# An attention block in split float32: who makes the lo parts of the weights, the squares of the outputs, and the product with the gate

## The chip, the cores and the metric

The kernel runs on one core of one Trainium2 chip. The metric is the device time of the whole program in microseconds, the median of several executions. A profiled execution also leaves a trace with every instruction of the five engines: TensorE (PE, with its weight loads as PEld), VectorE (DVE), ScalarE (ACT), GpSimd (POOL) and SyncE (SP, which only issues transfers here).

## What is computed

One transformer block over 512 tokens of width 2048, in float32. A projection of the normed input gives the inputs of four groups of 8 heads each: a latent attention (MLA), a causal attention with forget gates (FoX), a sparse attention with three branches (NSA) and a sliding window with sinks (SWA). Their outputs are normed by group, projected by `w_out` and added to the input; an MLP with a squared ReLU and a last norm follow. Cut to what matters here:

```python
def nsa_mixer(...):
    o_cmp, o_sel = nsa_cmp_sel(qg, k_cmp, v_cmp, ksl, vsl, tbl)
    o_win = banded_attention(qg, kwn, vwn, NSA_WINDOW, tbl)
    gts = jax.nn.sigmoid(gate).reshape(b, t, g, r, 3).transpose(0, 2, 3, 1, 4)
    o = gts[..., 0:1] * o_cmp + gts[..., 1:2] * o_sel + gts[..., 2:3] * o_win

def reference(...):
    u = rmsnorm(h, norm_attn[l])
    p = jnp.split(u @ w_in[l], offsets, axis=-1)
    ...
    o = jnp.concatenate([o_mla, o_fox, o_nsa, o_swa], axis=-1).reshape(b, t, N_GROUPS, GROUP_WIDTH)
    o = rmsnorm(o, group_norm[l].reshape(N_GROUPS, GROUP_WIDTH)).reshape(b, t, MIX_WIDTH)
    h = h + o @ w_out[l]
    m = rmsnorm(h, norm_mlp[l]) @ w_up[l]
    h = h + jnp.square(jax.nn.relu(m)) @ w_down[l]
    return rmsnorm(h, final_norm)
```

## The kernel before

A float32 product is made of three products in a shorter float format: each factor x is split into hi (x rounded to that format) and lo (x - hi, rounded again), and TensorE adds hi·hi, hi·lo and lo·hi in PSUM.

Weights come in pieces. `piece` (line 204) takes a raw tile of 128 x 1024 from a transfer on SyncE's queue (three raw buffers), lets ScalarE cast it to `hi` (line 210), and lets the engine in `lo_engine` subtract to get `lo` (line 211). `hi` and `lo` have two buffers each, in the arena `hl`. `lo_engine` is VectorE for the first projections (until about 115 us) and GpSimd from line 604 on. That holds 82 pieces: the projections to queries, keys and values that run inside the attention, and the output projection.

The attention runs as a list of steps, one for each block of 128 queries of a head, in the order MLA, NSA, FoX, SWA. TensorE's order is written out by hand: scores of step i, some products of a projection that has been cut in small portions (`pull`), transposes of the probabilities of step i-1 (line 565), more portions, and the values of step i-2 (line 571). The order of the other engines is left to a planner that follows the dependencies with a cost model; `nc.any` copies (line 518) go to VectorE or ScalarE as the planner sees fit. Every engine works through its queue in order.

`soft` (line 497) makes the probabilities: VectorE adds the bias to the scores in PSUM and finds the negated maximum `nm` (line 503), ScalarE takes the exponential with its sum `l` (line 506), VectorE takes the reciprocal `r` (line 511), multiplies it by the gate (through the helper `tt`, line 136) where the branch has one, and scales the row by it (line 514). Two branches of the NSA pass a gate, 64 blocks in all. The compressed branch has code of its own.

`finish_head` copies a head's output to `oT`; after the second head of a pair `add_squares` (line 529) squares the pair's tile of 128 x 512 and adds it to its group's sum `sqs`, on GpSimd. `group_rstd` reads the sum some steps into a later phase. There are 16 such tiles in four groups, so 16 squares and 12 additions.

GpSimd's queue holds besides these a few masks and the transfers that carry the residual to and from DRAM (lines 1249 and 1345).

Of the kernel before, what the change touches and what calls it, by code (L numbers as in the profile page):

```python
# [10 lines left out]
F32 = mybir.dt.float32  # L11
F32R = mybir.dt.float32r
BF16 = mybir.dt.bfloat16
AF = mybir.ActivationFunctionType
ALU = mybir.AluOpType
# [60 lines left out]
def block(tc, a, out):  # L76
    nc = tc.nc
    pool = tc.tile_pool
    with (
# [29 lines left out]
        def tl(shape, dt, tag, bufs=1):  # L109
            if tag not in plan:  # L110
                return sb.tile(shape, dt, tag=tag, name=tag, bufs=bufs)
            slots, size, used = plan[tag]
            arena, off = slots[used[0] % len(slots)]
            off //= 4
            used[0] += 1
            free = list(shape[1:])
            m = math.prod(free)
            assert (2 if dt == BF16 else 4) * m <= size, tag
            if dt == BF16:
                t = arena[0:shape[0], off:off + m // 2].bitcast(BF16)  # L120
            else:
                assert dt == arena.dtype, tag
                t = arena[0:shape[0], off:off + m]
            if len(free) == 2:
                t = t.rearrange("p (a b) -> p a b", b=free[1])
            elif len(free) == 3:
                t = t.rearrange("p (a b c) -> p a b c", b=free[1], c=free[2])
            elif len(free) == 4:
                t = t.rearrange("p (a b c d) -> p a b c d", b=free[1], c=free[2], d=free[3])
            return t  # L130
# [4 lines left out]
        def tt(o, x, y, op):  # L135
            nc.vector.tensor_tensor(o, x, y, op=op)  # L136
# [48 lines left out]
        def small(shape, tag, bufs=4):  # L185
            return tl(shape, F32, tag, bufs)
# [12 lines left out]
            return y  # L199


        lo_engine = [nc.vector]

        def piece(fills, used=1024):
            raw = tl([P, 1024], F32, "raw")
            for f in fills:
                f(raw)
            hi = tl([P, 1024], F32R, "hi")
            lo = tl([P, 1024], F32R, "lo")
            nc.scalar.copy(hi[:, 0:used], raw[:, 0:used])  # L210
            lo_engine[0].tensor_tensor(lo[:, 0:used], raw[:, 0:used], hi[:, 0:used].bitcast(F32), op=ALU.subtract)  # L211
            return hi, lo

        def w_piece(w, r0, kt, c0, n):

            def fill(raw):
                nc.sync.dma_start(raw[:, 0:kt * n].rearrange("p (k c) -> p k c", c=n),
                                  w[r0:r0 + kt * P, c0:c0 + n].rearrange("(k p) c -> p k c", p=P))
            return piece([fill], kt * n)
# [43 lines left out]
        def proj_tok(segs, n, before=lambda pc: None):  # L263

            accs = [ps("acc") for _ in range(TB)]
            for pc in range(8):
                before(pc)
                def fill(raw, pc=pc):
                    off = 0
                    r = raw[:, 0:2 * n].rearrange("p (k c) -> p k c", c=n)  # L270
                    for c0, w in segs:
                        nc.sync.dma_start(r[:, :, off:off + w],
                                          w_in[pc * 256:(pc + 1) * 256, c0:c0 + w].rearrange("(k p) c -> p k c", p=P))
                        off += w
                wh, wl = piece([fill], 2 * n)
                for b in range(TB):
                    for k in range(2):
                        kt = pc * 2 + k
                        for j, (w, u) in enumerate(three(wh, wl, uh[kt], ul[kt])):
                            mm(accs[b][:, 0:n], lhsT=u[:, b * P:(b + 1) * P], rhs=w[:, k * n:(k + 1) * n],  # L280
                               start=(kt == 0 and j == 0), stop=(kt == KT - 1 and j == 2))
            return accs
# [40 lines left out]
        for k in range(4):  # L323
            t = ps("s")
            for b in range(TB):
# [4 lines left out]
                                           op1=ALU.subtract)  # L330
# [166 lines left out]
        def soft(S, W, bias, sink=None, mul=None):  # L497

            p = tl([P, 512], F32, "tp")
            nm = small([P, 1], "nm")  # L500
            l = small([P, 1], "l")
            r = small([P, 1], "r")
            nc.vector.tensor_tensor_reduce(p[:, 0:W], S[:, 0:W], bias, scale=-1.0,  # L503
                                           scalar=big if sink is None else sink[1], op0=ALU.add, op1=ALU.min,
                                           accum_out=nm)
            nc.scalar.activation(p[:, 0:W], p[:, 0:W], AF.Exp, bias=nm, scale=-1.0, accum_out=l)  # L506
            if sink is not None:
                e = small([P, 1], "es")
                nc.scalar.activation(e, sink[0], AF.Exp, bias=nm)
                tt(l, l, e, ALU.add)  # L510
            nc.vector.reciprocal(r, l)
            if mul is not None:
                tt(r, r, mul, ALU.mult)
            nc.vector.tensor_scalar_mul(p[:, 0:W], p[:, 0:W], r)  # L514
            return p

        def evac(o, i):
# [2 lines left out]
        oT = [None] * 16  # L520
        sqs = {}
# [7 lines left out]
        def add_squares(n):  # L529

            if n % 4 == 0:
                sqs[n // 4] = tl([P, T], F32, "sqs")
                nc.gpsimd.tensor_tensor(sqs[n // 4], oT[n], oT[n], op=ALU.mult)
            else:
                sq = tl([P, T], F32, "tp")
                nc.gpsimd.tensor_tensor(sq, oT[n], oT[n], op=ALU.mult)
                nc.gpsimd.tensor_tensor(sqs[n // 4], sqs[n // 4], sq, op=ALU.add)

        def group_rstd(g):

# [60 lines left out]
        def fill_v(raw):  # L601
            nc.sync.dma_start(raw[:, 0:512].rearrange("p (h c) -> p h c", c=64), w_ukv_h[:, :, 64:128])
        wh, wl = piece([fill_v], 512)
        lo_engine[0] = nc.gpsimd
        vm = tl([P, TB, 512], F32, "acc2")
        for b in range(TB):
            acc = ps("acc")
# [61 lines left out]
        def mla_head(h):  # L669
            def score(i):  # L670
                W = (i + 1) * P

                def f(head):
                    Qh, Ql, Kh, Kl = kept[f"mla{h}"]
                    S = ps("s")
                    for j, (q, k) in enumerate(three(Qh, Ql, Kh, Kl)):
                        mm(S[:, 0:W], lhsT=q[:, i * P:W], rhs=k[:, 0:W], start=(j == 0), stop=(j == 2))
                    return soft(S, W, causal[:, 512 - W:512])
                return Block(f, W, lambda kb: vm[:, kb, h * 64:(h + 1) * 64], range(i + 1), i, 3 * W / 2.4)

            return Head(h // 2, h % 2, [score(i) for i in range(TB)], lambda: require(f"mla{h}"))
# [445 lines left out]
        with tc.manual_schedule(engines={mybir.EngineType.PE}):  # L1127
# [5 lines left out]
            for i in range(len(steps) + 2):  # L1133
# [15 lines left out]
                if i >= 2:  # L1149
                    head, _, j = steps[i - 2][:3]  # L1150
                    n = len(head.blocks)
# [289 lines left out]
        for j0, j1 in zip(GROUPS, GROUPS[1:]):  # L1441
            n, ms = j1 - j0, ready
# [115 lines left out]
```

## Time and profile before

| | |
|---|---|
| median of 3 executions | 2196.44 us (2195.49 to 2198.48) |
| profiled execution, its own time | 2199.35 us |
| span of the profile, first to last instruction | 2197.6 us |
| mean granted TensorE clock | 0.994 |
| PE busy | 2139.2 us, 97% |
| DVE busy | 1685.0 us, 77% |
| ACT busy | 1013.5 us, 46% |
| POOL busy | 247.8 us, 11% |

Busy times are of one profiled execution. An engine's instruction is busy from its start to its end, also while something outside it holds it up. TensorE's ends are modelled. A granted clock of 1.00 is 2.4 GHz, one of 0.50 is 1.2 GHz. Times in the rows count from the first instruction.

### The profile page before, as it was taken

The numbers are of one execution on the slowest core, as the hardware profiler recorded it, in microseconds if no ns is written. First come the engines' busy times: TensorE is split into PE (matmuls) and PEld (weight loads), VectorE is DVE, ScalarE is ACT, GpSimd is POOL, SyncE is SP. The second block draws the span as 40 slices with busy tenths as digits, with TensorE's granted clock in tenths as the row PEclk, the third lists the DMA queues.
The fourth block names the chain that finished last, engine by engine and source line by source line (L and its number), as shares of the span: only waits on it lengthen the run. The fifth ranks groups of instructions, "written<-read, shape, count | busy, mean of one in ns | idle before, by whom it ended". The sixth has DMA issues, their size and how long they took to land.

```text
span 2197.6 us, 37520 instructions
## 1 busy us (share of the span) xinstructions
PE 2139.2 (97%) x14441; PEld 1927.2 (88%) x14441; DVE 1685.0 (77%) x3118; ACT 1013.5 (46%) x1646; POOL 247.8 (11%) x152
## 2 busy tenths in 40 slices
PE   8999999999999998999999999999999999999998
PEld 6778777777778787999999999999999999999996
DVE  3466755665576657888888888888788888889997
ACT  4354433434455525654444444446544444444434
POOL 0011322323333343100000000000000000000000
PEclk9999999999999999999999999999999999999999
DMA  6452222222233233655544544456544544544553
GB/s 184 119 152 70 76 61 78 68 71 76 69 120 101 68 96 128 200 186 165 164 163 145 167 164 163 143 167 221 192 131 153 176 139 150 175 142 147 169 178 114
DMA packets 244815, 299.27 MB, mean 136 GB/s; under 512 B 28268, under 2 KB 199327, under 8 KB 239900
## 3 DMA queue, kind: packets, MB, share of 16 engines
q1 hardware_dynamic: 231424, 246.60, 37.4%
q10 hardware_dynamic: 11228, 41.87, 4.9%
q0 software_dynamic: 1984, 8.41, 1.1%
q8 instruction: 113, 1.85, 0.3%
q14 instruction: 66, 0.54, 0.1%
HBM read 254.70 MB, written 49.46 MB: 138 GB/s over the span
## 4 chain that ended last, share of the span: by engine, by line
PE 82%; DVE 9%; DMA 3%; issue 3%; ACT 2%; POOL 0%; ACTq 0%; SPq 0%; DVEq 0%; POOLq 0%
PE acc L1293 22%; PE s L1293 13%; PE acc L423 9%; PE t L1293 6%; PE acc L973 6%; PE acc L1397 4%; PE acc L280 4%; PE o L571 3%; PE o L1293 3%; PE s L1397 2%; PE acc L894 2%; PE t L565 2%; DVE tpp L514 1%; PE o L1397 1%; PE t L1397 1%
## 5 line engine op out<-in xcount | busy, mean ns | idle before, releaser
L423 PE MATMUL acc<-u,hl 128*128 128x512 f32 x1008 | 282.0, 411 | 0.0
L211 POOL TENSOR_TENSOR hl<-raw,hl 128x1024 fp32r<-128x1024 f32 x82 | 197.3, 2406 | 456.6 <-ACT hl L210 394.7
L1293 PE MATMUL acc<-u,acc 128*128 128x256 f32 x1162 | 233.2, 281 | 0.6 <-DVE ka L1400 0.6
L1287 ACT CAST acc<-raw 128x896 fp32r<-128x896 f32 x146 | 136.7, 941 | 178.5 <-PE t L1293 79.6
L1287 ACT CAST acc<-bx 128x896 fp32r<-128x896 f32 x146 | 136.8, 941 | 173.2 <-PE acc L1293 71.1
L1287 ACT CAST acc<-tpp 128x896 fp32r<-128x896 f32 x144 | 134.7, 941 | 175.9 <-PE acc L1293 70.5
L423 PEld LDWEIGHTS acc<-u,hl 128*128 128x128 f32 x1008 | 177.4, 191 | 34.5 <-issue 4.8
L973 PE MATMUL acc<-hl,u 128*128 128x512 f32 x768 | 195.0, 401 | 5.0 <-DVE acc L981 2.3
L1293 PEld LDWEIGHTS acc<-u,acc 128*128 128x128 f32 x1162 | 186.5, 188 | 1.0 <-DVE ka L1400 0.8
L506 ACT ACTIVATE tpp<-tpp,nm 128x256 f32<-128x256 f32 (+3 forms) x160 | 86.5, 541 | 184.9 <-DVE nm L503 176.1
L973 PEld LDWEIGHTS acc<-hl,u 128*128 128x128 f32 x768 | 139.2, 189 | 35.5 <-DVE acc L981 3.0
L210 ACT CAST hl<-raw 128x1024 fp32r<-128x1024 f32 (+2 forms) x99 | 102.3, 1033 | 136.7 <-PE acc L973 46.3
L1293 PE MATMUL acc<-ot,acc 128*128 128x256 f32 x714 | 152.1, 283 | 3.4 <-ACT acc L1287 3.4
L1293 PE MATMUL s<-u,acc 128*128 128x256 f32 x664 | 134.6, 281 | 0.0
L1293 PE MATMUL acc<-acc,acc 128*128 128x256 f32 x476 | 133.8, 281 | 0.0
L1293 PEld LDWEIGHTS acc<-ot,acc 128*128 128x128 f32 x714 | 118.3, 190 | 3.8 <-ACT acc L1287 3.6
L136 DVE TENSOR_TENSOR bx<-bx 128x256 f32<-128x256 f32 (+1 forms) x219 | 111.6, 510 | 11.6 <-DMA bx<-in_w_up_dram 4.3
L136 DVE TENSOR_TENSOR tpp<-tpp 128x256 f32<-128x256 f32 (+1 forms) x222 | 114.6, 517 | 6.5 <-DMA tpp<-in_w_up_dram 1.9
L136 DVE TENSOR_TENSOR raw<-raw 128x256 f32<-128x256 f32 (+1 forms) x219 | 111.6, 509 | 9.4 <-DMA raw<-in_w_down_dram 5.6
L1293 PEld LDWEIGHTS s<-u,acc 128*128 128x128 f32 x664 | 106.4, 188 | 0.0
L1293 PE MATMUL acc<-u,u 128*128 128x256 f32 x371 | 103.9, 280 | 0.0
L1288 DVE TENSOR_TENSOR ot<-raw,acc 128x896 fp32r<-128x896 f32 x72 | 78.1, 1088 | 20.2 <-ACT acc L1287 20.2
(683 smaller groups left out, 5946.3 us busy)
## 6 DMA issues: line engine op xcount, KB each, us to landing
m_dram<-ka ACTq DMA_DIRECT2D x32, 1024.0 KB, 5.2
raw<-in_w_in_dram SPq DMA_DIRECT2D x58, 512.0 KB, 3.9
bx<-in_w_up_dram SPq DMA_DIRECT2D x86, 256.0 KB, 2.8
raw<-in_w_up_dram SPq DMA_DIRECT2D x86, 256.0 KB, 2.8
tpp<-in_w_up_dram SPq DMA_DIRECT2D x84, 256.0 KB, 2.9
raw<-in_w_out_dram SPq DMA_DIRECT2D x32, 512.0 KB, 3.7
raw<-m_dram SPq DMA_DIRECT2D x30, 512.0 KB, 4.5
kb<-m_dram SPq DMA_DIRECT2D x30, 512.0 KB, 3.9
```

What stands on the lines that cost most here:

```text
L136: nc.vector.tensor_tensor(o, x, y, op=op)
L210: nc.scalar.copy(hi[:, 0:used], raw[:, 0:used])
L211: lo_engine[0].tensor_tensor(lo[:, 0:used], raw[:, 0:used], hi[:, 0:used].bitcast(F32), op=ALU.subtract)
L280: mm(accs[b][:, 0:n], lhsT=u[:, b * P:(b + 1) * P], rhs=w[:, k * n:(k + 1) * n], start=(kt == 0 and j == 0), stop=(kt == KT - 1 and j == 2))
L423: mm(acc[0], lhsT=x[:, k * P:(k + 1) * P], rhs=u, start=(kt == 0 and j == 0), stop=(kt == KT - 1 and j == 2))
L506: nc.scalar.activation(p[:, 0:W], p[:, 0:W], AF.Exp, bias=nm, scale=-1.0, accum_out=l)
L571: mm(o[r0:r0 + 64, self.i * P:(self.i + 1) * P], lhsT=self.V(kb), rhs=self.pt[:, j * P:(j + 1) * P], start=(first and j == 0), stop=(last ...
L973: mm(accs[b], lhsT=u[:, b * P:(b + 1) * P], rhs=x[:, k * 512:(k + 1) * 512], start=(hf == 0 and k == 0 and j == 0), stop=(hf == 1 and k == ...
L1287: nc.scalar.copy(wh, w[:, k, 0:7, :])
L1288: lo = nc.vector.tensor_tensor(wl, w[:, k, 0:7, :], wh.bitcast(F32), op=ALU.subtract)
L1293: mm(banks[bank][:, half * HT:(half + 1) * HT], lhsT=lhs, rhs=rhs, start=(start and k == 0 and i == 0 and half == 0), stop=(stop and k == ...
L1397: mm(acc, lhsT=y, rhs=x, start=(start and i == 0), stop=(stop and i == 2))
```

## The change

Three edits. The lo parts of all pieces are subtracted on VectorE, each in halves of up to 512 columns, and `lo_engine` goes. The squares of `add_squares` are taken by ScalarE and the additions by VectorE; GpSimd is left with masks, small copies and transfers. Where `soft` is given a gate, the reciprocal is no longer multiplied by it; the scaling takes both scalars, p · r · gate, in one instruction.

```diff
-        lo_engine = [nc.vector]
-
         def piece(fills, used=1024):
...
             nc.scalar.copy(hi[:, 0:used], raw[:, 0:used])
-            lo_engine[0].tensor_tensor(lo[:, 0:used], raw[:, 0:used], hi[:, 0:used].bitcast(F32), op=ALU.subtract)
+            for c in range(0, used, 512):
+                e = min(c + 512, used)
+                tt(lo[:, c:e], raw[:, c:e], hi[:, c:e].bitcast(F32), ALU.subtract)
             return hi, lo
...
             nc.vector.reciprocal(r, l)
-            if mul is not None:
-                tt(r, r, mul, ALU.mult)
-            nc.vector.tensor_scalar_mul(p[:, 0:W], p[:, 0:W], r)
+            if mul is None:
+                nc.vector.tensor_scalar_mul(p[:, 0:W], p[:, 0:W], r)
+            else:
+                nc.vector.tensor_scalar(p[:, 0:W], p[:, 0:W], r, mul, op0=ALU.mult, op1=ALU.mult)
             return p
...
             if n % 4 == 0:
                 sqs[n // 4] = tl([P, T], F32, "sqs")
-                nc.gpsimd.tensor_tensor(sqs[n // 4], oT[n], oT[n], op=ALU.mult)
+                nc.scalar.activation(sqs[n // 4], oT[n], AF.Square)
             else:
                 sq = tl([P, T], F32, "tp")
-                nc.gpsimd.tensor_tensor(sq, oT[n], oT[n], op=ALU.mult)
-                nc.gpsimd.tensor_tensor(sqs[n // 4], sqs[n // 4], sq, op=ALU.add)
+                nc.scalar.activation(sq, oT[n], AF.Square)
+                tt(sqs[n // 4], sqs[n // 4], sq, ALU.add)
...
         wh, wl = piece([fill_v], 512)
-        lo_engine[0] = nc.gpsimd
         vm = tl([P, TB, 512], F32, "acc2")
```

## Rows read from the trace of the kernel before

**Rows 1.** The page, parts 1 and 4: busy time of TensorE's matmuls (share of the span, instructions), and the shares of the engines in the chain of work that ended last.

```profile
PE 2139.2 (97%) x14441; PEld 1927.2 (88%) x14441; DVE 1685.0 (77%) x3118; ACT 1013.5 (46%) x1646; POOL 247.8 (11%) x152
...
PE 82%; DVE 9%; DMA 3%; issue 3%; ACT 2%; POOL 0%; ACTq 0%; SPq 0%; DVEq 0%; POOLq 0%
```

**Rows 2.** Busy time by stage. Columns: stretch, its length, then busy us and number of instructions for PE, PEld, DVE, ACT and POOL, then the granted TensorE clock as a share of full speed, the DMA engines' share, GB/s. The first four stretches are the attention by its phases, the fifth lies in the output projection, the last is the MLP.

```profile
124.00:260.00 136.00, 128.07 (x724) 105.49 (x723) 90.62 (x240) 61.14 (x153) 29.82 (x19) 0.97 0.35 93
260.00:440.00 180.00, 175.75 (x929) 138.71 (x928) 107.59 (x312) 73.17 (x163) 53.93 (x25) 0.99 0.26 70
440.00:645.00 205.00, 194.83 (x1066) 155.61 (x1067) 130.93 (x329) 92.50 (x202) 63.37 (x31) 1.00 0.29 82
645.00:770.00 125.00, 118.83 (x629) 97.17 (x628) 85.92 (x228) 65.96 (x180) 45.90 (x23) 1.00 0.29 88
...
840.00:860.00 20.00, 16.06 (x75) 12.29 (x74) 16.58 (x20) 9.44 (x14) 9.06 (x6) 0.98 0.21 74
...
905.00:2197.00 1292.00, 1280.41 (x9910) 1235.49 (x9908) 1128.10 (x1772) 606.46 (x741) 1.64 (x3) 1.00 0.50 162
```

**Rows 3.** TensorE's waits between 124 and 770 us: who waited for whom, us in total, times, the longest.

```profile
PE t L565 <- DVE tpp L514: 23.9, 18, 2.5
PE t L824 <- DVE r L136: 1.9, 2, 1.2
```

**Rows 4.** Groups of VectorE's and GpSimd's instructions by line and tile: count | busy us, mean ns | idle time of the engine before them. Line 136 is the helper `tt`, line 514 the scaling of probabilities.

```profile
L514 DVE TENSOR_SCALAR tpp<-tpp,r 128x256 f32<-128x256 f32 (+3 forms) x160 | 85.7, 536 | 4.0
...
L136 DVE TENSOR_TENSOR r<-r,gate 128x1 f32<-128x1 f32 x64 | 31.7, 496 | 1.8
...
L136 DVE TENSOR_TENSOR q<-ot,q 64x512 fp32r<-64x512 f32 x16 | 21.1, 1320 | 1.2 <-ACT q L459 0.7
...
L211 POOL TENSOR_TENSOR hl<-raw,hl 128x1024 fp32r<-128x1024 f32 x82 | 197.3, 2406 | 456.6 <-ACT hl L210 394.7 <-PE s L790 22.1 <-PE acc L423 20.8
```

**Rows 5.** Extremes of some of these instructions: count, least / median / greatest ns, first and last start in us, forms. The row of line 211 on VectorE holds the pieces of the first 124 us.

```profile
L136 DVE TENSOR_TENSOR r<-r,gate x64: 147/160/1876, 260.4 to 516.2; 128x1 f32<-128x1 f32 x64
...
L136 DVE TENSOR_TENSOR q<-ot,q x16: 677/687/2560, 246.5 to 703.9; 64x512 fp32r<-64x512 f32 x16
...
L514 DVE TENSOR_SCALAR tpp<-tpp,r x160: 270/382/2592, 128.5 to 768.8; 128x256 f32<-128x256 f32 x56, 128x128 f32<-128x128 f32 x40, 128x384 f32<-128x384 f32 x40, 128x512 f32<-128x512 f32 x24
...
L503 DVE CUSTOM_DVE_ANT_0 tpp<-s,bx,big x80: 333/541/751, 126.8 to 641.9; 128x384 f32<-128x384 f32 x24, 128x128 f32<-128x128 f32 x20, 128x256 f32<-128x256 f32 x20, 128x512 f32<-128x512 f32 x16
...
L211 DVE TENSOR_TENSOR hl<-raw,hl x17: 691/1093/1226, 11.6 to 113.4; 128x1024 fp32r<-128x1024 f32 x8, 128x896 fp32r<-128x896 f32 x8, 128x512 fp32r<-128x512 f32 x1
```

**Rows 6.** Instructions in order of time around 657 us, in the phase of the sliding windows: start us, us, engine, line, operation, tile; in brackets the idle time of the engine before it and what ended it.

```profile
653.35 0.34 DVE L514 TENSOR_SCALAR tpp<-tpp,r 128x256 f32<-128x256 f32 x1
...
655.48 1.03 ACT L210 CAST hl<-raw 128x1024 fp32r<-128x1024 f32 x1
...
656.58 2.52 DVE L514 TENSOR_SCALAR tpp<-tpp,r 128x256 f32<-128x256 f32 x1
656.59 2.36 POOL L211 TENSOR_TENSOR hl<-raw,hl 128x1024 fp32r<-128x1024 f32 x1 [3.71 <-ACT hl L210]
...
659.24 0.41 PE L565 MATMUL t<-ident,tpp 128*128 128x128 f32 x2 [1.75 <-DVE tpp L514]
```

**Rows 7.** The same view around 317 us, in the phase with the gate.

```profile
314.38 1.05 ACT L210 CAST hl<-raw 128x1024 fp32r<-128x1024 f32 x1 [2.50 <-issue]
...
316.07 0.16 DVE L511 RECIPROCAL r<-l 128x1 f32<-128x1 f32 x1 [0.63 <-ACT tpp L506]
...
316.26 1.64 DVE L136 TENSOR_TENSOR r<-r,gate 128x1 f32<-128x1 f32 x1
...
318.36 0.41 DVE L514 TENSOR_SCALAR tpp<-tpp,r 128x384 f32<-128x384 f32 x1
...
318.92 0.52 PE L565 MATMUL t<-ident,tpp 128*128 128x128 f32 x3 [1.74 <-DVE tpp L514]
```

**Rows 8.** Busy time as in rows 2, in short stretches; the granted clock is the third value from the end.

```profile
156.00:159.00 3.00, 3.00 (x14) 2.57 (x13) 2.74 (x7) 1.96 (x6) 0.14 (x1) 0.50 0.09 22
...
252.00:254.00 2.00, 2.00 (x8) 1.71 (x8) 0.76 (x4) 0.00 (x0) 0.00 (x0) 0.50 0.33 116
...
385.00:388.00 3.00, 3.00 (x10) 2.32 (x9) 0.91 (x4) 0.69 (x2) 0.00 (x0) 0.50 0.18 59
...
659.00:663.00 4.00, 3.76 (x23) 3.35 (x24) 3.22 (x15) 1.77 (x8) 0.00 (x0) 1.00 0.53 168
```

**Rows 9.** TensorE's own instructions in order of time, ahead of the first two of these stretches.

```profile
154.80 0.63 PE L565 MATMUL t<-ident,tpp 128*128 128x128 f32 x4 [2.23 <-DVE tpp L514]
...
251.03 0.52 PE L565 MATMUL t<-ident,tpp 128*128 128x128 f32 x3 [2.46 <-DVE tpp L514]
```

**Rows 10.** TensorE's instructions in the output projection.

```profile
857.15 0.49 PE L973 MATMUL acc<-hl,u 128*128 128x512 f32 x1 [1.73 <-POOL hl L211]
858.96 1.60 PE L973 MATMUL acc<-hl,u 128*128 128x512 f32 x3 [1.32 <-DVE acc L981]
```

**Rows 11.** ScalarE: the squares of the residual (line 983) as a group, and the waits of the cast that makes the hi parts (line 210) between 124 and 770 us.

```profile
L983 ACT ACTIVATE acc<-acc 128x512 f32<-128x512 f32 x12 | 7.2, 597 | 2.6 <-DVE acc L981 2.2 <-DVE l L136 0.2
...
ACT hl L210 <- issue: 24.4, 17, 3.6
...
ACT hl L210 <- PE acc L423: 8.9, 10, 2.0
```

## The prediction

> **What bounds the kernel now.** I read the page's busy shares and chain first, then a table by stage, then TensorE's waits, and then the neighbourhood of single waits. The page [rows 1] shows a kernel that is already TensorE's: it is busy for 97% of the span, and 82% of the chain that ended last lies on it. A change to VectorE, ScalarE and GpSimd can win only what TensorE stands idle for or does at a lower clock. The table by stage [rows 2] says where that is. From 905 us to the end (the MLP, which the diff does not touch) TensorE is busy for 1280.41 of 1292 us. In the attention, from 124 to 770 us, it is idle for 7.9, 4.3, 10.2 and 6.2 us of the four stages, 28.5 us together, and for 3.9 us more in the 20 us from 840. That is the purse.
>
> TensorE's waits say who holds it [rows 3]: 23.9 us in 18 waits for the scaling of probabilities (line 514) and hardly anything else. So I asked why that scaling is late. By the grouped instructions and their extremes [rows 4, 5] it takes 382 ns at the median but up to 2592. The multiplication by the gate, one element a partition, takes 160 ns at the median, 1876 at most and 496 on average. The lo parts of the queries take 687 and up to 2560. All three read SBUF alone. Single waits show the cause: in [rows 6] the scaling of 128x256 took 0.34 us at 653.35, and at 656.58 the same form took 2.52 us, since a GpSimd subtraction of lo parts began at 656.59 and ran for 2.36. They ended within 0.15 us of each other, and TensorE had waited 1.75 us. In [rows 7] the gate's multiplication hung 1.64 us in the same way. The 82 subtractions on GpSimd, 2406 ns each [rows 4], are thus no work beside VectorE but a hold on it; VectorE's own busy time is in part waiting.
>
> The clock is a second, smaller item [rows 8]. In three stretches the granted clock was 0.50, which is 1.2 instead of 2.4 GHz; ahead of the first two TensorE had paused for 2.23 and 2.46 us [rows 9]; behind the 1.75 us of [rows 6] the clock stayed at 1.00.
>
> **The change part by part.**
>
> *Lo parts on VectorE in halves.* Removed: 82 GpSimd subtractions, 197.3 us of GpSimd, and the hold. Added: 164 VectorE subtractions of 128x512. The row that holds VectorE's own line 211 has 691 ns as its least, and its one 128x512 form is in it [rows 5], so 164 x 0.691 = 113.3 us. Against it VectorE loses the gate's multiplications (31.7 us), the stretched part of the scalings (85.7 us less 160 x 0.382 = 61.1, so 24.6) and of the query parts (21.1 less 16 x 0.687, so 10.1) [rows 4, 5]: 66.4 us. With the 12 additions below, the net is 113.3 + 8.3 - 66.4 = 55 us more on VectorE at most, over 734 us. The attention's stages, 60 to 69% busy now [rows 2], would be at 67 to 77%. VectorE's sum thus does not fall; what falls is the longest thing that can stand in a probability's way, from 2.4 us to 1.38 (two halves) or 0.69 (one).
>
> What that is worth I get by timing two waits again. In [rows 6] the cast ended at 655.48 + 1.03 = 656.51. If both halves run ahead of the scaling, it ends at 656.51 + 1.38 + 0.34 = 658.23, and with the 0.14 us that TensorE took to answer it starts at 658.37, not 659.24: 0.87 of 1.75 us is saved. If the scaling slips in front, all 1.75 is. In [rows 7] the cast ended at 315.43 and the halves would end at 316.81; a reciprocal (0.16) and the scaling (0.41) end at 317.38. TensorE starts at 317.52 instead of 318.92: 1.40 of 1.74 us saved at the least. The two lower bounds are 2.27 of 3.49 us, 65%. So the 23.9 us shrink by 15.5 to 23.9. I take 18, nearer to the lower end, because nothing on the page says that a scaling will slip in front.
>
> *What queues behind the halves.* A half waits for the cast on ScalarE (line 210), and behind it on VectorE wait the negated maximum (line 503), the reciprocal and the scaling of the current block, for which ScalarE's exponential and then TensorE's transposes wait. GpSimd does not hold line 503, which reads its scores from PSUM and never took over 751 ns [rows 5]; a half does. So there will be waits that before does not have. No row shows them. From below none; from above as many as now, 18 of 0.3 to 0.9 us, which is 11 us. I take 4.
>
> *The clock.* The three stretches lose at least half of 3 + 2 + 3 us [rows 8], 4.0 us. The pauses ahead of the first two would lose 0.87 or more and then be shorter than the 1.75 us behind which the clock stayed up. I count 4; none to 5.
>
> *Output projection.* At 857 us TensorE waits 1.73 us for a GpSimd subtraction and 1.32 us for an addition of VectorE's [rows 10]. VectorE is busy for 16.58 of these 20 us [rows 2], and gets 3 x 1.38 us more for what it loses in holds. I count 1.5 of the 3.05 us; 0 to 3.
>
> *Squares.* Sixteen move from GpSimd to ScalarE, where the nearest row, a square of the same shape with an accumulated sum, takes 597 ns [rows 11]: 9.6 us on an engine that is 41 to 53% busy in these stages [rows 2]. Twelve additions go to VectorE at the halves' 0.69 us, 8.3 us, counted above. Their result is wanted some steps later, so this is hidden; with that cover gone it would cost 16 x 0.6 = 9.6 us, where each delays an exponential. I take 1. That square runs between exponentials already, so no new table is brought in.
>
> *The gate in the scaling.* 64 instructions fall away, 0.16 us each in the chain when unheld. The scaling with two scalars isn't in the trace at this width. From below it costs nothing more; from above, it may lose the rate by which the 128x384 form takes 0.41 us: a subtraction of 128x512 takes 0.69, and by its columns 384 would take some 0.52. That is 0.11 more, which the 0.16 pays for. I take nothing either way.
>
> **The sum.** -18 - 4 - 1.5 + 4 + 1 = -18.5 us. The profiled execution took 2199.35 us (span 2197.6), 2.9 above the median of 2196.44; to the median the same difference is applied: **2178 us**.
>
> **Rivals.** Bound for all: 0.2%, or 4.4 us, is about what a measurement of this kernel can tell from no change.
>
> *Smaller gain.* The halves always run first, new waits come to their upper bound, and the clock still falls: -15.5 - 1.5 + 11 + 1 = -5 us, 2191. For it: VectorE gets fuller, not emptier. Against it: the shortest chains have room, for at least 64 of the 82 subtractions now make no wait at line 514 [rows 3].
>
> *VectorE becomes the bound; no change.* VectorE at 77% with all work in one queue delays as many chains as the hold did: 30 new waits of 0.6 us eat the 18.5, 2196. The trace now has room: the fullest attention stage is 69% busy, holds included [rows 2]. The Trainium skill, "Perfetto Trace Analysis", section on optimizing Scalar and DVE operations, speaks for this rival: a saturated VectorE may gain from giving work to ScalarE or even GpSimd, and the change does the opposite. The same section warns that these two share a read port, so that moving work between them might not help; [rows 6] agree with that warning, at 2.52 us in place of 0.34.
>
> *Slower: VectorE stands behind the cast.* ScalarE's cast waits at the head of its queue for a free buffer: 24.4 us in 17 waits plus 8.9 in 10 [rows 11]. GpSimd could idle meanwhile. A half that sits early in VectorE's queue stands there too, and a maximum and a scaling stand behind it until the cast (1.05 us) and both halves (1.38) are through, 2.4 us. If 27 such places each cost TensorE 1.2 us, that is 32 us against a gain of 18.5: 2210. It decides from 0.7 us a place. Against it: while ScalarE stands at the cast it makes no exponentials either, so most of these stalls are there now without a row of TensorE's.
>
> *Larger gain.* The scaling slips in front everywhere and nothing new waits: -23.9 - 5 - 3 = -32 us, 2164.
>
> **How the numbers follow.** Chances: forecast with its surroundings (2167 to 2186) 0.48; larger gain 0.12; smaller gain 0.18; no change 0.10; slower 0.12. The predicted time is the likeliest one's, 2178. The range reaches from just below the larger gain, 2162, to 2198, the upper side of no change; beyond it lie most of the slower rival and a little at the low end. Faster by over 0.2%: 0.48 + 0.12 + 0.18 = 0.78; same 0.10; slower 0.12.
>
> **What would show it.** Right: no VectorE scaling over 0.7 us, TensorE's waits for it under 10 us, the granted clock at 1.00 around 156, 252 and 386 us, GpSimd near idle, VectorE's busy time up by 20 to 55 us, no new long wait of VectorE for the cast, and the MLP as long as before. Wrong: VectorE waiting for line 210 by tens of us, TensorE's waits moved to the negated maximum or the evacuations, or a tail from 840 to 905 us that has grown, since VectorE is at its fullest there.

## The result and the profile after

The changed kernel takes 2168.42 us (median, 2167.92 to 2174.55), the kernel before, beside it on the chip, 2197.46. The ratio is 0.987, with a 95% interval of 0.985 to 0.990: 29 us less, where I had said 18.5. The profiled executions, 2199.35 and 2168.01 us, lie 31.3 apart, and the stages below are of these.

First the page of the changed kernel, busy times and chain, as in [rows 1].

```profile
PE 2128.8 (98%) x14441; PEld 1923.8 (89%) x14441; DVE 1683.6 (78%) x3230; ACT 1026.0 (47%) x1678; POOL 17.4 (1%) x42
...
PE 86%; DVE 5%; DMA 4%; issue 2%; ACT 2%; SPq 0%; ACTq 0%; DVEq 0%; POOLq 0%
```

With the same 14441 matmuls TensorE is busy for 10.4 us less than in [rows 1], and it is idle for 37.5 us where it was 58.4 (span less busy time). VectorE's share of the chain went from 9 to 5%. GpSimd is all but empty. VectorE has 112 instructions more and is busy for just as long as before: 164 halves, 16 more from the halving of the first pieces and 12 additions came, 64 products with the gate went, and the planner moved 16 of its `nc.any` copies to ScalarE.

To put stages beside each other they have to hold the same work, so here both kernels are cut at the same instructions: the first scores of MLA, NSA and FoX, FoX's last product with the mask, the last transpose of probabilities, the first product of the MLP. Columns as in [rows 2]. The kernel before:

```profile
124.80:253.00 128.20, 120.27 (x679) 99.05 (x679) 86.93 (x228) 59.61 (x149) 28.77 (x18) 0.98 0.37 98
253.00:516.50 263.50, 253.93 (x1352) 201.14 (x1351) 161.54 (x462) 103.58 (x231) 75.55 (x35) 0.99 0.26 69
516.50:640.30 123.80, 119.54 (x664) 96.12 (x663) 75.47 (x182) 61.74 (x132) 40.55 (x21) 1.00 0.30 86
640.30:769.40 129.10, 122.34 (x645) 99.93 (x645) 89.73 (x235) 67.26 (x182) 47.35 (x24) 1.00 0.29 89
769.40:871.60 102.20, 97.00 (x446) 78.28 (x447) 62.40 (x94) 36.61 (x52) 39.94 (x21) 0.98 0.35 113
871.60:1118.10 246.50, 241.15 (x2016) 240.33 (x2015) 218.03 (x353) 131.09 (x173) 8.21 (x15) 0.99 0.53 175
1118.10:2197.60 1079.50, 1067.58 (x8118) 1022.86 (x8116) 940.22 (x1465) 498.08 (x613) 0.00 (x0) 1.00 0.50 160
```

The changed kernel:

```profile
125.20:250.00 124.80, 118.24 (x679) 97.10 (x679) 86.24 (x250) 60.23 (x152) 0.41 (x2) 1.00 0.38 99
250.00:502.50 252.50, 250.70 (x1353) 199.42 (x1352) 154.31 (x453) 105.99 (x237) 0.00 (x0) 1.00 0.27 72
502.50:622.00 119.50, 118.41 (x665) 96.50 (x664) 77.73 (x209) 65.97 (x142) 0.00 (x0) 1.00 0.32 91
622.00:743.80 121.80, 121.61 (x645) 100.09 (x645) 87.91 (x261) 72.23 (x195) 0.00 (x0) 1.00 0.30 95
743.80:840.20 96.40, 94.00 (x448) 77.28 (x448) 69.55 (x125) 37.59 (x52) 2.75 (x5) 1.00 0.37 120
840.20:1085.90 245.70, 241.41 (x2016) 240.41 (x2015) 216.62 (x353) 130.64 (x172) 8.21 (x15) 0.99 0.54 175
1085.90:2166.30 1080.40, 1067.93 (x8118) 1022.99 (x8116) 939.95 (x1465) 497.93 (x613) 0.00 (x0) 1.00 0.50 160
```

The stages are 3.4, 11.0, 4.3, 7.3 and 5.8 us shorter, 31.8 in all, and the MLP is the same within 0.1 us. Stage length less PE busy gives the idle time: 33.7 us over the first five before, 12.0 after. So of the 31.8 us 21.7 were TensorE's idle time and 10.1 its busy time. In the sliding windows (622 to 743.8) TensorE now pauses for 0.2 us in 122.

What TensorE still waits for between 124 and 744 us, as in [rows 3]:

```profile
PE t L566 <- DVE tpp L513: 5.7, 7, 1.9
PE t L566 <- ACT kb L519: 1.1, 1, 1.1
PE t L824 <- DVE tpp L136: 1.1, 2, 0.6
PE s L677 <- DVE q L136: 1.0, 1, 1.0
PE t L566 <- DVE tpp L515: 0.7, 4, 0.2
```

The scaling is now line 513, and 515 where it takes the gate. The 23.9 us of [rows 3] are 6.4.

The extremes of VectorE's instructions, as in [rows 5] (least, median, greatest ns):

```profile
L513 DVE TENSOR_SCALAR tpp<-tpp,r x96: 276/353/487, 128.6 to 743.2; 128x256 f32<-128x256 f32 x40, 128x128 f32<-128x128 f32 x24, 128x384 f32<-128x384 f32 x16, 128x512 f32<-128x512 f32 x16
...
L515 DVE TENSOR_SCALAR tpp<-tpp,r,gate x64: 322/444/547, 256.6 to 503.0; 128x384 f32<-128x384 f32 x24, 128x128 f32<-128x128 f32 x16, 128x256 f32<-128x256 f32 x16, 128x512 f32<-128x512 f32 x8
...
L136 DVE TENSOR_TENSOR q<-ot,q x16: 677/686/690, 246.0 to 684.9; 64x512 fp32r<-64x512 f32 x16
...
L136 DVE TENSOR_TENSOR hl<-raw,hl x192: 189/684/695, 122.7 to 830.0; 128x512 fp32r<-128x512 f32 x164, 128x48 fp32r<-128x48 f32 x14, 128x288 fp32r<-128x288 f32 x7, 128x64 fp32r<-128x64 f32 x7
```

What reached 2592, 2592 and 2560 ns in [rows 5] now ends at 487, 547 and 690. That is the hold, gone.

The clock, as in [rows 8], in the places that answer to its dips, and last in the one dip that is left near them. It lies behind the five stages; the kernel before had one there too, at 890 us.

```profile
155.00:160.00 5.00, 4.16 (x30) 3.21 (x28) 3.02 (x9) 2.83 (x9) 0.12 (x1) 1.00 0.12 29
246.00:250.00 4.00, 2.13 (x11) 1.52 (x10) 3.20 (x9) 1.18 (x5) 0.00 (x0) 1.00 0.69 174
384.00:388.00 4.00, 4.00 (x21) 3.31 (x20) 2.95 (x8) 0.80 (x3) 0.00 (x0) 1.00 0.26 52
...
855.00:859.00 4.00, 3.60 (x17) 3.60 (x18) 3.96 (x6) 3.05 (x7) 1.10 (x2) 0.58 0.22 61
```

Finally, a halved lo part and a scaling in one place, in the sliding windows, as in [rows 6]:

```profile
636.09 1.05 ACT L208 CAST hl<-raw 128x1024 fp32r<-128x1024 f32 x1
...
637.00 0.34 DVE L513 TENSOR_SCALAR tpp<-tpp,r 128x256 f32<-128x256 f32 x1
...
637.26 1.28 DVE L136 TENSOR_TENSOR hl<-raw,hl 128x512 fp32r<-128x512 f32 x2
...
638.22 0.38 PE L566 MATMUL t<-ident,tpp 128*128 128x128 f32 x2
```

The scaling stands in front of the halves, took 0.34 us, and TensorE's transposes followed with no pause ahead of them.

### The profile page after: what moved, and what is told of

The parts are those of the page before. It is cut to its first block, busy times and chain, and to the rows that moved or that the text cites. A ratio compares the mean times of both kernels' runs of the same rounds, so it can differ in the third digit from the quotient of the medians.

```text
span 2166.3 us, 37497 instructions
## 1 busy us (share of the span) xinstructions
PE 2128.8 (98%) x14441; PEld 1923.8 (89%) x14441; DVE 1683.6 (78%) x3230; ACT 1026.0 (47%) x1678; POOL 17.4 (1%) x42
## 4 chain that ended last, share of the span: by engine, by line
PE 86%; DVE 5%; DMA 4%; issue 2%; ACT 2%; SPq 0%; ACTq 0%; DVEq 0%; POOLq 0%
PE acc L1293 23%; PE s L1293 13%; PE acc L423 10%; PE acc L973 7%; PE t L1293 6%; PE acc L1397 4%; PE o L572 4%; PE o L1293 3%; PE acc L280 3%; PE s L1397 2%; PE acc L894 2%; PE t L566 2%; PE s L790 1%; PE o L1397 1%; PE t L1397 1%
## 5 line engine op out<-in xcount | busy, mean ns | idle before, releaser
L136 DVE TENSOR_TENSOR hl<-raw,hl 128x512 fp32r<-128x512 f32 (+3 forms) x235 | 143.3, 637 | 93.0 <-ACT hl L208 85.9
L506 ACT ACTIVATE tpp<-tpp,nm 128x256 f32<-128x256 f32 (+3 forms) x160 | 86.4, 540 | 137.2 <-DVE nm L503 133.2
L136 DVE TENSOR_TENSOR bx<-bx 128x256 f32<-128x256 f32 (+1 forms) x219 | 111.5, 509 | 13.1 <-DMA bx<-in_w_up_dram 6.4
L1288 DVE TENSOR_TENSOR ot<-tpp,acc 128x896 fp32r<-128x896 f32 x72 | 78.0, 1087 | 20.2 <-ACT acc L1287 20.2
```

Of the source, the lines that this page charges most:

```text
L1288: lo = nc.vector.tensor_tensor(wl, w[:, k, 0:7, :], wh.bitcast(F32), op=ALU.subtract)
```

## The experiments

The theory was that GpSimd's subtractions hold VectorE, and that the time came back with the hold. The first rival was that the new order of VectorE's and ScalarE's queues did it, or one of the two smaller edits. The second was about size: that VectorE's added work costs much and hides a larger gain. Medians in us, and the ratio to the kernel before, measured beside it, with its 95% interval:

| kernel | median | ratio |
|---|---|---|
| before + lo parts alone | 2172.71 | 0.989 (0.987 to 0.990) |
| before + gate alone | 2192.54 | 0.997 (0.996 to 0.998) |
| before + squares alone | 2198.02 | 1.000 (0.999 to 1.001) |
| after + hold | 2207.13 | 1.004 (1.003 to 1.006) |
| after without lo parts | 2155.30 | 0.981 (0.979 to 0.982) |
| after + memsets | 2170.25 | 0.988 (0.986 to 0.989) |
| after, copies on ScalarE | 2169.32 | 0.987 (0.986 to 0.989) |
| after, lo in one, first time | 2171.24 | 0.988 (0.987 to 0.990) |
| after, lo in one, again | 2169.74 | 0.987 (0.985 to 0.989) |
| after, lo in quarters | 2170.89 | 0.988 (0.986 to 0.989) |
| after as it is, again | 2168.75 | 0.987 (0.985 to 0.988) |

The runs were taken in three sets, each on one chip; the kernel before had medians of 2197.61, 2198.67 and 2198.17 us in them.

### Each edit alone

**The lo parts alone**, in the kernel before:

```diff
-            lo_engine[0].tensor_tensor(lo[:, 0:used], raw[:, 0:used], hi[:, 0:used].bitcast(F32), op=ALU.subtract)
+            for c in range(0, used, 512):
+                e = min(c + 512, used)
+                tt(lo[:, c:e], raw[:, c:e], hi[:, c:e].bitcast(F32), ALU.subtract)
```

> The kernel before, with one of the three edits: the lo parts on VectorE in halves. Squares stay on GpSimd, the gate keeps its own multiplication. If the hold of GpSimd's subtractions on VectorE is the cause, this brings nearly all of the gain: 24 to 28 of the 28 us, so a ratio of 0.987 to 0.989 to the kernel before (some 2169 to 2174 us); what is left are 28 GpSimd instructions of 1.0 to 1.3 us that still hold VectorE. If the shorter chain of the gate is the cause, the gain is under half: above 2183 us.

24.9 us less than before, as expected of the hold. This edit carries most of the change.

**The gate alone:**

```diff
-            if mul is not None:
-                tt(r, r, mul, ALU.mult)
-            nc.vector.tensor_scalar_mul(p[:, 0:W], p[:, 0:W], r)
+            if mul is None:
+                nc.vector.tensor_scalar_mul(p[:, 0:W], p[:, 0:W], r)
+            else:
+                nc.vector.tensor_scalar(p[:, 0:W], p[:, 0:W], r, mul, op0=ALU.mult, op1=ALU.mult)
```

> The kernel before, with one of the three edits: the scaling takes the reciprocal and the gate together. GpSimd keeps the lo parts and the squares. If GpSimd's hold is the cause, it now catches the scaling where it caught the gate's multiplication, and only the 64 short instructions are saved: 0 to 4 us faster than the kernel before, 2193 to 2198 us. If the shorter chain were the cause, 10 us or more: below 2187 us.

6.1 us less (3.7 to 8.1 by the interval): more than the 0 to 4 that I expected, less than the 10 of the rival. The stage of the gate, NSA, in this kernel, and two of the stretches in which the clock was at half before:

```profile
252.20:508.90 256.70, 250.72 (x1353) 199.59 (x1353) 149.05 (x397) 103.63 (x231) 74.90 (x35) 1.00 0.26 71
...
251.00:255.00 4.00, 4.00 (x24) 3.41 (x24) 3.01 (x9) 0.70 (x3) 0.00 (x0) 1.00 0.37 107
384.00:388.00 4.00, 4.00 (x27) 3.29 (x26) 1.22 (x6) 2.52 (x5) 1.83 (x2) 1.00 0.00 0
```

The stage is 6.8 us shorter than before, the other four together by about 1. Idle time fell from 9.6 to 6.0 us, and the two clock dips, at the stage's start and inside it, are gone. The hold is still there in this kernel (its two-scalar scaling takes up to 1943 ns). That a chain with one instruction fewer has one place fewer to be caught in is my reading; no run tests it.

**The squares alone:**

```diff
-                nc.gpsimd.tensor_tensor(sqs[n // 4], oT[n], oT[n], op=ALU.mult)
+                nc.scalar.activation(sqs[n // 4], oT[n], AF.Square)
...
-                nc.gpsimd.tensor_tensor(sq, oT[n], oT[n], op=ALU.mult)
-                nc.gpsimd.tensor_tensor(sqs[n // 4], sqs[n // 4], sq, op=ALU.add)
+                nc.scalar.activation(sq, oT[n], AF.Square)
+                tt(sqs[n // 4], sqs[n // 4], sq, ALU.add)
```

> The kernel before, with one of the three edits: the squares on ScalarE and their additions on VectorE. GpSimd keeps the lo parts. If GpSimd's hold is the cause, this removes 28 of its 110 instructions and 33 of its 230 us in the attention, so about a seventh of the hold: 1 to 5 us faster, 2192 to 2197 us. If it is ScalarE's time that counts, up to 5 us slower.

No change that can be measured: 0.7 us less by the medians. The 1 to 5 us that I expected of a seventh of the hold don't show. The three edits alone add to 24.9 + 6.1 + 0.7 = 31.7 us, the whole to 29.0; the difference lies inside the intervals, so whether they add up exactly is open.

### The hold put back

GpSimd gets a subtraction of the same size as before behind the halves; its result is used by nothing. VectorE's and ScalarE's queues hold the same instructions in the same order as in the changed kernel.

```diff
                 tt(lo[:, c:e], raw[:, c:e], hi[:, c:e].bitcast(F32), ALU.subtract)
+            if held[0]:
+                nc.gpsimd.tensor_tensor(raw[:, 0:used], raw[:, 0:used], hi[:, 0:used].bitcast(F32), op=ALU.subtract)
             return hi, lo
...
         wh, wl = piece([fill_v], 512)
+        held[0] = True
```

> The changed kernel, and after the two halves of each of the 82 pieces GpSimd subtracts hi from the raw tile once more, in place, which nothing reads. VectorE, ScalarE and TensorE have the same instructions in the same order as in the changed kernel; GpSimd again has 82 subtractions of 2.4 us. If GpSimd holds VectorE while both read SBUF, the long scalings (up to 2.5 us) and TensorE's waits for them come back and all of the gain goes, perhaps more, since VectorE now has the 113 us as well: 2193 to 2215 us. If the gain came from lo parts that are ready sooner, or from another order of the queues, the time stays at that of the changed kernel, 2166 to 2173 us.

38.7 us slower than the changed kernel, and 9.5 slower than the one before. Its page, and the group of the added subtraction (columns as in [rows 4]):

```profile
PE 2139.0 (97%) x14441; PEld 1927.1 (87%) x14441; DVE 1767.4 (80%) x3230; ACT 1024.4 (47%) x1678; POOL 220.1 (10%) x124
...
L215 POOL TENSOR_TENSOR raw<-raw,hl 128x1024 f32<-128x1024 f32 x82 | 202.6, 2470 | 520.0 <-DVE hl L136 366.8 <-DVE l L136 18.9 <-ACT ot L472 17.2
```

VectorE has its 3230 instructions as in the changed kernel and is busy with them for 83.8 us longer. TensorE's waits from 124 to 776 us:

```profile
PE t L570 <- DVE tpp L517: 16.3, 18, 3.9
PE t L829 <- DVE tpp L136: 7.2, 3, 2.7
...
PE t L570 <- DVE tpp L519: 2.8, 8, 0.7
```

The two scalings make 18 waits of 16.3 us and 8 of 2.8, 19.1 together, where [rows 3] has 23.9; the compressed branch (line 829) adds 7.2 where it had 1.9. The order of the queues is excluded as the cause: in the two traces every one of VectorE's 3230, ScalarE's 1678 and TensorE's 14441 instructions stands at the same place in its queue. The added subtraction also keeps the raw tile in use for longer. The memsets below do that too, for some 2 us a piece, and cost next to nothing, so that doesn't explain the time either. In the output projection the stage takes 103.0 us here, 102.2 before, 96.4 after; that gain too is the hold's.

### What VectorE's own work still costs

The 82 pieces from line 604 on get no lo part at all, so part of the computation is left out: TensorE does the same products with whatever the buffers hold.

```diff
+        lo_made = [True]
...
-            for c in range(0, used, 512):
+            for c in range(0, used, 512) if lo_made[0] else ():
...
         wh, wl = piece([fill_v], 512)
+        lo_made[0] = False
```

> The changed kernel without the lo subtractions of the 82 pieces inside the attention and the output projection: the lo buffers keep what earlier pieces left there, so this leaves out part of the computation. It takes 113 us of work off VectorE and puts it nowhere. If VectorE's room in the attention is enough, TensorE wins at most the 6 to 10 us that it still waits there: 2158 to 2168 us. If VectorE has become a bound, more: below 2155 us.

2155.30 us, 13.1 less than the changed kernel: more than the 10 us of the first expectation, and just short of the second. Not all of it need be VectorE's work, since the planner also gave 14 copies back to VectorE here, so the queues differ. The stages, cut at the same instructions as above, without FoX and the sliding windows, in which TensorE is busy for the whole of 118.2 and 121.4 us:

```profile
125.80:245.30 119.50, 117.92 (x679) 97.15 (x679) 74.01 (x227) 61.65 (x154) 0.43 (x2) 1.00 0.38 102
245.30:495.00 249.70, 249.70 (x1353) 200.12 (x1352) 126.00 (x403) 104.59 (x232) 0.00 (x0) 1.00 0.27 74
...
734.60:828.80 94.20, 93.94 (x448) 77.18 (x447) 51.82 (x95) 37.02 (x53) 2.75 (x5) 1.00 0.37 119
```

TensorE is idle for 1.8 us in 703. This is close to the floor of these stages with TensorE's work as it is; the changed kernel stands 12 us above it, 5.3 of them in MLA.

With the hold and without the lo parts on VectorE (the kernel before) it is 2197; with neither, 2155; with the lo parts alone, 2168; with both, 2207. So the subtraction costs 39 us (2207 less 2168) to 42 (2197 less 2155) as a hold, and 10 (2207 less 2197) to 13 (2168 less 2155) as work of VectorE. The kernel before also differs in gate and squares, so the 39 is the cleaner figure of the hold.

### Reading and writing on GpSimd

In place of the subtraction two useless memsets of the raw tile, which read nothing:

```diff
+            if held[0]:
+                for _ in range(2):
+                    nc.gpsimd.memset(raw[:, 0:used], 0.0)
             return hi, lo
```

> The changed kernel with two GpSimd memsets of the raw tile after the halves of each of the 82 pieces, some 2.1 us together, which nothing reads. VectorE, ScalarE and TensorE have the same instructions in the same order as in the changed kernel. These GpSimd instructions write SBUF and read nothing. The Trainium skill, SBUF - State Buffer, section on who interferes with whom, says that a VectorE instruction in a 2-port mode is blocked by any GpSimd instruction, one with two SBUF inputs only by one that reads. By that the scalings are stretched by up to 2.1 us and the lo parts of the queries are not. From the rows of the run with the useless subtraction, where the hold cost 39 us and the scalings were about half of what was stretched: 2175 to 2195 us. If only reading holds VectorE, as the changed kernel, 2166 to 2173 us.

1.8 us slower than the changed kernel by the medians, with intervals that overlap. The 2175 to 2195 us that I had derived for stretched scalings missed: they are stretched, as the rows show, and the time hardly moves. The memsets as a group, then extremes in this kernel:

```profile
L216 POOL MEMSET raw<- 128x1024 f32 x164 | 160.2, 978 | 526.4 <-issue 208.1 <-DVE hl L136 52.0 <-ACT q L464 46.0
...
L518 DVE TENSOR_SCALAR tpp<-tpp,r x96: 277/354/1265, 128.4 to 743.0; 128x256 f32<-128x256 f32 x40, 128x128 f32<-128x128 f32 x24, 128x384 f32<-128x384 f32 x16, 128x512 f32<-128x512 f32 x16
...
L136 DVE TENSOR_TENSOR q<-ot,q x16: 675/686/687, 244.8 to 684.7; 64x512 fp32r<-64x512 f32 x16
...
L136 DVE TENSOR_TENSOR l<-l,es x32: 143/158/163, 626.4 to 742.6; 128x1 f32<-128x1 f32 x32
```

The same three in the kernel with the subtraction:

```profile
L517 DVE TENSOR_SCALAR tpp<-tpp,r x96: 277/353/2486, 128.4 to 773.5; 128x256 f32<-128x256 f32 x40, 128x128 f32<-128x128 f32 x24, 128x384 f32<-128x384 f32 x16, 128x512 f32<-128x512 f32 x16
...
L136 DVE TENSOR_TENSOR q<-ot,q x16: 677/1395/2795, 245.6 to 711.9; 64x512 fp32r<-64x512 f32 x16
L136 DVE TENSOR_TENSOR l<-l,es x32: 144/160/2290, 649.9 to 773.1; 128x1 f32<-128x1 f32 x32
```

Against a memset the scalings stretch, and so do a few other VectorE operations on one tensor in SBUF (a cast of 64x512 took 1243 ns, 420 at the least); the operations with two inputs in SBUF keep their times. Against the subtraction both kinds stretch. The reciprocal, one element a partition and one input, took at most 167 ns in each of these kernels and in the one before. The Trainium skill, "SBUF — State Buffer", section Who interferes with whom, says just this: an operation with two SBUF inputs is blocked by a GpSimd instruction that reads SBUF and not by one that only writes, and one in a two-port mode by either. The rows agree, though none shows which mode a scaling runs in. The times do not compare like for like, since a memset lasts 0.98 us and the subtraction 2.47, and a memset holds fewer kinds of instruction: 164 memsets cost 1.8 us, if anything, where 82 subtractions cost 39.

### One, two or four pieces; who copies

The lo part in one instruction of VectorE, and in quarters:

```diff
-            for c in range(0, used, 512):
-                e = min(c + 512, used)
-                tt(lo[:, c:e], raw[:, c:e], hi[:, c:e].bitcast(F32), ALU.subtract)
+            tt(lo[:, 0:used], raw[:, 0:used], hi[:, 0:used].bitcast(F32), ALU.subtract)
```

```diff
-            for c in range(0, used, 512):
-                e = min(c + 512, used)
+            for c in range(0, used, 256):
+                e = min(c + 256, used)
```

> The changed kernel, but the lo part of a piece in one VectorE instruction of 1.22 us instead of two of 0.69. If it matters that a scaling can slip between the halves, 4 to 8 us slower than the changed kernel (2172 to 2176 us). If the halves run back to back in any case, or the room of the chains is more than 1.2 us, within 2 us of it (2166 to 2170 us), and VectorE is busy for 13 us less.

> The changed kernel with the lo parts subtracted in quarters of up to 256 columns. By the medians of the halves (684 ns for 512 columns) and of the whole in one (1222 ns for 1024) a quarter takes about 415 ns, so a piece takes 1.66 us of VectorE where the halves take 1.37 and the whole 1.22: 24 us more on VectorE over the 82 pieces. Theory that the longest single instruction ahead of a scaling matters: about 1 us faster than the halves of the same call (the same order of gain as from the whole to the halves). Theory that VectorE's sum matters, since leaving the subtraction out gave 13 us for 112 us of VectorE, 0.12 us for each us: 24 x 0.12 = 3 us slower than the halves. Theory that only the hold counted and the rest is slack: within 1 us.

> The changed kernel as it is, on the chip of the quarters and of the whole: about 2168 us, ratio 0.987, as the yardstick for both.

> The changed kernel with the lo part in one VectorE instruction, again, beside the halves on one chip. If length matters, 2 to 3 us slower than the halves, as the medians of the first time had it; if VectorE's sum matters, 12 us less of it give 1.5 us faster; if neither, within 1 us.

On one chip 2169.74, 2168.75 and 2170.89 us for one, two and four. The differences, 1.0 and 2.1 us, lie inside the intervals; one instruction had been 2.8 us behind the first time and is 1.0 behind now. By the medians halving is worth 1 to 3 us, and whether it is worth anything stays open.

**The copies on ScalarE.** As VectorE's work still costs 13 us, its copies out of PSUM (63 of them, chosen by the planner) were given to ScalarE:

```diff
         def evac(o, i):
-            nc.any.tensor_copy(o, i)
+            nc.scalar.copy(o, i)
```

> The changed kernel, with the copies of transposed probabilities and of head outputs from PSUM always on ScalarE instead of where the planner sees fit. That takes some 80 copies of 0.3 to 0.7 us, about 30 us, off VectorE and gives them to ScalarE, which is less busy. Leaving the lo parts out had shown 13 us still to be won from VectorE's queue. If VectorE's queue is what is left, 2 to 6 us faster than the changed kernel, 2162 to 2166 us. If ScalarE's exponentials now stand behind the copies, as long or up to 6 us slower, 2168 to 2175 us.

2169.32 us, no change, as the second expectation had it. VectorE's busy time fell to 1663.3 us and nothing came of it. ScalarE took the copies over, so this run can't tell whether VectorE's sum costs nothing or ScalarE's new work ate the gain. Single halves ahead of single scalings are another reading of the 13 us, and it isn't shown. In the changed kernel it fits the longest wait for a scaling:

```profile
244.67 1.29 DVE L136 TENSOR_TENSOR hl<-raw,hl 128x512 fp32r<-128x512 f32 x2
...
248.16 0.41 DVE L513 TENSOR_SCALAR tpp<-tpp,r 128x384 f32<-128x384 f32 x1
...
248.72 0.52 PE L566 MATMUL t<-ident,tpp 128*128 128x128 f32 x3 [1.87 <-DVE tpp L513]
```

VectorE works from the halves to this scaling with no pause over 0.04 us. It does not fit the next three (at 160.62, 193.77 and 226.64 us, 3.0 us together): there VectorE sits idle for over a microsecond ahead of the reciprocal, waiting for ScalarE's exponential, and no half comes between. No version that does the whole computation beat the changed kernel.

## Why the prediction was right, and where it was off

**The mechanism** was right and is shown: with the hold put back and the queues in the same order, 38.7 us return. The size was not: 18.5 us forecast, 29.0 measured. The time lies in the stated range, and near the low edge of the forecast's own surroundings. It is not a case of errors that cancel, for nearly all of them made the gain too small.

**Scaling waits, -18 (15.5 to 23.9).** Measured 23.9 less 6.4, -17.5. I had taken the lower end plus a little, since nothing told that a scaling would slip in front; the timeline at 637 us shows one that did. But a half that delays a scaling ends in this same row, as at 248.72 us above, so old waits saved and new ones made can't be told apart in it.

**New waits behind the halves, +4 (0 to 11).** None to speak of. In the waits list of after each of the others is 1.1 us or less, and the idle time of the first four stages fell from 28.5 to 9.6 us, which is more than the scalings' own 17.5. As a term beside the scalings' it should have been 0. The wait that I feared exists, between 124 and 744 us:

```profile
DVE hl L136 <- ACT hl L208: 25.6, 27, 2.4
...
ACT tpp L506 <- DVE nm L503: 133.2, 82, 2.4
```

VectorE stands behind the cast for 25.6 us in 27 places, by chance the very number of the slower rival, and no row of TensorE's list answers to it. That ScalarE makes no exponentials then either, as I had argued, fits; no run tests it. ScalarE's wait for the negated maximum fell from 176.1 us in 96 waits, in the same view of before, to 133.2 in 82: these waits did not grow.

**The clock, -4 (0 to 5).** Too small, and outside its range. I counted three stretches at 0.50 and took the middles of them, 2 to 3 us. Cut with their edges, the dips of the kernel before are these:

```profile
155.00:160.00 5.00, 5.00 (x27) 4.36 (x26) 4.50 (x10) 2.94 (x8) 0.14 (x1) 0.66 0.15 36
251.00:255.00 4.00, 3.97 (x14) 3.41 (x15) 2.07 (x7) 0.46 (x2) 0.00 (x0) 0.57 0.39 116
384.00:388.00 4.00, 4.00 (x16) 3.27 (x15) 1.66 (x7) 0.69 (x2) 0.00 (x0) 0.57 0.42 132
859.00:863.00 4.00, 4.00 (x13) 3.23 (x14) 4.00 (x5) 0.00 (x0) 0.54 (x1) 0.57 0.73 246
```

Length times (1 - clock) is 1.7 us each, and there were four: the fourth, in the output projection, had left its mark in [rows 2] (0.98 from 840 to 860). That is 6.9 us, all of it gone from the five stages. Their busy time fell by 10.1; the other 3.2 us I can't assign. With the hold put back TensorE's busy time over the whole kernel was 2139.0 us again, so they too hang on it in some way.

**Output projection, -1.5 (0 to 3).** Too small as well. The stage gave 5.8 us: 1.7 by the clock dip just named, 2.8 of idle time (5.2 to 2.4), and 1.3 of the unassigned busy time. I had looked at 3.05 us in two waits of a stage that was idle for 5.2.

**Squares, +1.** 0.7 us less than before when alone, inside its interval. A square takes 0.62 us on ScalarE, near the 597 ns of [rows 11].

**The gate, 0.** Right for the instruction, wrong for the edit. The two-scalar form takes 342, 410, 477 and 544 ns for 128 to 512 columns, and the one-scalar form 285, 350, 419 and 481: some 60 ns more at any width, so it keeps the rate. But alone the edit gave 6.1 us. I had priced 0.16 us for the instruction that falls away; in [rows 4] it took 0.50 on average because it was held, and that I had entered in VectorE's budget and not in the chain. How much it adds once the hold is gone is less clear: the changed kernel is 4.3 us ahead of the lo parts alone, in separate measurements whose intervals overlap.

**VectorE busier by up to 55 us.** Wrong: -1.4. Of the 120.5 us added (164 x 0.684 and 8.3) the three items that I had priced gave back 64.5 (31.7 + 85.7 + 21.1, less 63.0 and 11.0), as expected. The other 57 have three sources. Other held operations, which I had not looked at, got shorter; 16 copies went to ScalarE; and busy time counts two instructions that overlap once. Added up one by one, VectorE's instructions are 16.9 us longer than before, and 18.3 us more of them overlap. Of the holds: added up over every VectorE instruction of the kernel before that overlaps one of GpSimd's, time above the least of its form is 92.6 us; the kernel with the hold put back says 83.8. So the 82 subtractions cost VectorE about a microsecond each, and doing them itself costs 1.37 (two halves).

Of the signs that I named, these came: no scaling above 0.7 us, waits for it under 10, the clock at 1.00 in all three places, GpSimd near idle, the MLP unchanged. VectorE's busy time did not rise. A long wait for the cast did come, which I had named as a sign of being wrong, and the time shows no harm from it. With the terms as measured (-17.5, -6.9, -2.8) the sum is -27.2, or 2169 us, between the forecast and the "larger gain". The stages of the two profiles differ by 31.8: the 3.2 us of busy time and 1.4 of idle time have no term.

## What to carry to other kernels

Before an elementwise operation is left on GpSimd as free, look at the spread of VectorE's durations for one form: a median of 382 ns with a greatest of 2592 says that VectorE pays for it, and the sum of the excess over the least is about what it gets back, here three quarters of the work it then takes on. Whether the time follows is read from TensorE's waits. Price an instruction that falls away by what it took in the chain, held, and not by its least. Count clock dips with a window wide enough to hold their edges, in all stages, and count the queues' waits only where TensorE has a row for them.

## What was not expected of the hardware

An operation on one element a partition, with two inputs in SBUF, is held nearly as long as a wide one (2290 ns against 160, with the hold put back), while the reciprocal beside it, with one input, never took over 167, though 37 of its 160 in the kernel before ran wholly inside an instruction of GpSimd. A second scalar in the scaling costs some 60 ns at any of the four widths. And 160 us of memsets on GpSimd next to the same VectorE work cost 1.8 us by the medians, inside the noise, where 203 us of subtractions cost 39.
